# An encoder block on one core: Hyena products ahead of the conformer products, and five smaller changes of order

## The chip, the core and the metric

The kernel runs on one core of a Trainium2 chip. The metric is the device time of one execution in microseconds; before the change its median is 1410.63 us over three runs (1410.6 to 1410.8).

## The reference, cut to what matters

One layer on 256 tokens of width 2048, all in float32. `hy_*` and `cf_*` are the two branches, each of width 1024.

```python
h = rms_norm(x, mix_pre_g)
proj = h @ w_in                       # [hyena 3*1024 | cf_a | cf_b | gate_a | gate_b]
hy_in = depthwise_conv(hy_in, hy_conv_w, hy_conv_b)          # 3 taps
v, x1, x2 = split(hy_in)
kf = hyena_filters_freq(...)          # small MLP with sines, then a Fourier transform
z = x1 * fft_long_conv(v, kf[0]);  y_a = x2 * fft_long_conv(z, kf[1])
u = depthwise_conv(cf_a * sigmoid(cf_b), cf_dw_w, cf_dw_b)   # 31 taps
y_b = silu(layer_norm(u, cf_ln_g, cf_ln_b))
merged = sigmoid(gate_a) * (y_a @ hy_proj) + sigmoid(gate_b) * (y_b @ cf_proj)
x = x + rms_norm(merged @ w_out, mix_post_g)
h = rms_norm(x, ffn_pre_g)
x = x + rms_norm((silu(h @ w_gate) * (h @ w_up)) @ w_down, ffn_post_g)
```

## The kernel before, in words

**Products.** Every weight comes from memory once, in pieces of [128 x 2 x 512] (512 KB), by a load on SP's queue. `split_group` (line 281) lets ACT cast the piece to a rounded high part `hi` (line 299) and DVE subtract to get the low part `lo` (line 300). PE then does three products for each block of weights: activation high and low against `hi`, activation high against `lo`. There are four buffers for the raw piece and three each for `hi` and `lo`, so loads, splits and products of neighbouring groups overlap. All products go through the helper at line 87. `chunk_as` (line 355) makes a [256 x 512] result in two banks of PSUM, `main`: 8 groups of 12 products for a width of 2048, 4 groups for a width of 1024.

**Side work.** Everything else (filter, long convolutions, LayerNorm, evacuation of results) is written as generators. After each weight group the loop calls `pump(budget)` (line 108): it steps the generators in the queue until their stated costs use up the budget; `yield 1.2` states a cost, `yield None` ends the generator's turn until the next group. At most two of the generators in `side` are stepped in one turn. `drain` (line 134) steps given generators to their end at once. `before_chunk` and `after_chunk` keep at most one chunk's evacuation waiting. The program is then ordered by a scheduler (line 1246) that may move instructions where nothing pins them; `keep_in_program_order`, and `in_order` (line 197) for all calls on an engine, pin the instructions marked so among each other.

**Start.** Eight products of zeros run first (line 172) and one more in `first_chunk` (line 315), before the first weights. `x_norm` (line 459) loads x in four pieces, squares them on ACT (lines 272 and 469), forms rstd on DVE (`rsqrt`, line 223) and spreads it with a small product (line 450) to `rX`. `conv3` (line 724) needs `rX` to evacuate the first chunk (line 734). `filter_mlp` (line 496) waits six turns, loads five small arrays, and does two small products (lines 506 and 513), each followed by a sine (line 494).

**Middle.** After the six Hyena inputs and four conformer chunks come eight gate chunks (line 944), stored as sigmoids. Then, for each of four column chunks, the Hyena product (`hy_proj`), scaled by its gate (line 822), and the conformer product (`cf_proj`), merged with it (lines 928 and 929), transposed and split for the next product. The conformer branch ends at lines 863 and 867, and `layer_norm` (line 871) follows: statistics, rstd, normalization (line 881), and for each of four column pairs four transposes (line 892), sigmoid on ACT (line 899), an affine on DVE (line 900), a product (line 902), and the high and low part (lines 906 and 907) that `cf_proj` takes in. All that is left of `side` is drained behind the first Hyena product, in front of the first conformer product:

```python
    for n in range(4):
        before_chunk()
        after_chunk(scale_by(chunk_as(a["hy_proj"][n], yaT, 1.35), gates[n]))
        drain(side if n == 0 else [])
        before_chunk()
        mT.extend(slot([P, 2, 2, T], F32R) for _ in range(2))
        after_chunk(merge(chunk_as(a["cf_proj"][n], ybT, 1.35), gates[4 + n], gates[n], mT[-2:]))
```

**Products with a norm behind them.** `w_out` and `w_down` go through `product_as` (line 382): groups are one block of 128 rows and one half `hf` of the columns. The last eight groups (`late`) are split ahead into spare buffers, and their products are done token half by token half, piece by piece, so that each piece can be squared and scaled while the next is computed. After `w_out`, `turn` (line 1007) transposes the first token half, `turn_first` (line 1037) while the second half is still computed; `first_gate` (line 1064) starts the first FFN chunk with hand-placed products, and turns the second half in its loop, with `ahead` splitting weights ahead. `finish_block` (line 1136) writes the output in five pieces for each token half.

Of the kernel before, what the change touches and what calls it, by code (L numbers as in the profile page):

```python
# [15 lines left out]
ALU = mybir.AluOpType  # L16
AX = mybir.AxisListType

P = 128
# [34 lines left out]
def block_kernel(ctx: ExitStack, tc: tile.TileContext, a: dict, out: bass.AP):  # L54
# [248 lines left out]
    def first_chunk(act, budget, turn):  # L303


        ps = [psm.tile([P, 2, T], F32, tag="main", name=nm("main")) for _ in range(2)]
        kept = tc.keep_in_program_order
        groups = KT // 2
        ahead = deque()

        def split(g):
            ahead.append(split_group(a["w_in0"][g], on=(act_chain, dve_chain)))

        turn(0)
        keep_warm(1, zeros[:, 0:P], zeros)
        split(0)
        for g in range(groups):
            if g + 1 < groups:
                turn(g + 1)
                split(g + 1)  # L320
            hi, lo = ahead.popleft()
            for k in range(2):
                for c in range(4):
                    o = ps[c // 2][:, c % 2, :]
                    for s in range(2):
                        kept(mm(o, hi[:, k, c * P:(c + 1) * P], act[g][:, k, s, :],
                                g == 0 and k == 0 and s == 0 and c % 2 == 0, False))
            for k in range(2):
                for c in range(4):
                    kept(mm(ps[c // 2][:, c % 2, :], lo[:, k, c * P:(c + 1) * P],  # L330
                            act[g][:, k, 0, :], False, g == groups - 1 and k == 1))
            pump(budget)
        return ps
# [48 lines left out]
    def product_as(w, nkt, act, budget, late, done):  # L382

        ps = [[], []]
        first = 4
        groups = [(kt, hf) for hf in range(2) for kt in range(first)]
        groups += [(kt, hf) for kt in range(first, nkt) for hf in range(2)]

        def mms(kt, hf, t, hi, lo):
            av = act[kt // 2][:, kt % 2, :, t * P:(t + 1) * P]
            for j in range(2):
                o = ps[t][2 * hf + j]
                mm(o, av[:, 0, :], hi[:, j, :], kt == 0, False)
                mm(o, av[:, 1, :], hi[:, j, :], False, False)
            for j in range(2):
                mm(ps[t][2 * hf + j], av[:, 0, :], lo[:, j, :], False, kt == nkt - 1)

        held = []  # L400
        before_chunk()
        for i, (kt, hf) in enumerate(groups):
            if kt == 0:
                if hf:
                    drain(list(evac))
                    evac.clear()
                ps[0] += [aux() for _ in range(2)]
                ps[1] += [psm.tile([P, 512], F32, tag="main", name=nm("main")) for _ in range(2)]
            ahead = i >= len(groups) - late
            hi, lo = split_group(  # L410
                w[kt * P:(kt + 1) * P, hf * 1024:(hf + 1) * 1024].rearrange(
                    "p (j n) -> p j n", n=512), ahead)
            if ahead:
                held.append((kt, hf, hi, lo))
            else:
                for t in range(2):
                    mms(kt, hf, t, hi, lo)
                pump(budget)
        for t in range(2):
            for n in range(4):  # L420
                for kt, hf, hi, lo in held:
                    if hf == n // 2:
                        av = act[kt // 2][:, kt % 2, :, t * P:(t + 1) * P]
                        mm(ps[t][n], av[:, 0, :], hi[:, n % 2, :], False, False)
                        mm(ps[t][n], av[:, 1, :], hi[:, n % 2, :], False, False)
                        mm(ps[t][n], av[:, 0, :], lo[:, n % 2, :], False, kt == nkt - 1)
                done(t, n, ps[t][n])
# [29 lines left out]


    def x_norm():
        for _ in range(2):  # L460
            yield None
        for c in range(4):
            xs = slot([P, 2, 512])
            nc.sync.dma_start(
                xs, a["xm"][:, c * 512:(c + 1) * 512].rearrange("(t p) n -> p t n", p=P))
            for _ in range(2):
                yield None
            for t in range(2):
                tc.keep_in_program_order(half_mean_square(xs[:, t, :], ssx[:, t, c:c + 1]))
        yield 1.2  # L470
        for t in range(2):
            rms_rstd(rstd_x[:, t:t + 1], ssx[:, t, :], f"rx{t}")
        yield None
        per_token(rX, rstd_x, aux())
        done.add("x_norm")
# [18 lines left out]
        nc.scalar.activation(dst, u, AF.Sin)  # L494

    def filter_mlp():
        for _ in range(6):
            yield None
        nc.sync.dma_start(zT, a["zT"])
        nc.sync.dma_start(w1, a["w1"])  # L500
        nc.sync.dma_start(fp, a["fp"])
        for i in range(2):
            nc.sync.dma_start(w2d[:, i * FH:(i + 1) * FH], a["w2"])
        yield None
        ps = aux()
        tc.keep_in_program_order(nc.tensor.matmul(ps[:FH, :T], w1, zT, start=True, stop=True))
        h1 = scr[:FH, 2, :]
        sin_layer(h1, ps[:FH, :T], FH, 0)
        yield 1.9
        for _ in range(3):  # L510
            yield None
        ps = aux()
        tc.keep_in_program_order(nc.tensor.matmul(ps[:, :T], w2d, h1, start=True, stop=True))
        h2 = scr[:, 3, :]
        sin_layer(h2, ps[:, :T], P, 2)
        nc.scalar.copy(h2s, h2)
        nc.vector.tensor_tensor(out=h2s[FH:], in0=h2[FH:], in1=h2s[FH:], op=ALU.subtract)
        done.add("mlp")
        yield 2.2
# [351 lines left out]
    def layer_norm():  # L871
        while ("cf", 0) not in done or ("cf", 1) not in done:
            yield None
        for t in range(2):
            nc.vector.bn_aggr(out=mv[:, t, :], in_=stats[:, t])
        vv = sm([P, 2], "lnv", bufs=1)
        nc.vector.tensor_scalar(vv, mv[:, :, 1], EPS, 0.5, op0=ALU.add, op1=ALU.mult)
        rsqrt(rstd_c, vv, 2, "ln")
        yield 1.5
        for t in range(2):  # L880
            nc.vector.tensor_scalar(
                yt[t], yt[t], mv[:, t, 0:1], rstd_c[:, t:t + 1],
                op0=ALU.subtract, op1=ALU.mult)
            yield 0.6
        yield None
        yield from hold(3)
        for cp in range(4):
            ps = aux().rearrange("p (c t) -> p c t", t=T)
            for cc in range(2):
                c = 2 * cp + cc  # L890
                for t in range(2):
                    nc.tensor.transpose(
                        ps[:, cc, t * P:(t + 1) * P], yt[t][:, c * P:(c + 1) * P], ident)
            sg = t5([P, 2, T])
            lin = t5([P, 2, T])
            for cc in range(2):
                c = 2 * cp + cc
                g, b = pv[:, LN_G + c:LN_G + c + 1], pv[:, LN_B + c:LN_B + c + 1]
                nc.scalar.activation(sg[:, cc, :], ps[:, cc, :], AF.Sigmoid, bias=b, scale=g)
                nc.vector.tensor_scalar(lin[:, cc, :], ps[:, cc, :], g, b, op0=ALU.mult, op1=ALU.add)  # L900
            yb = t5([P, 2, T])
            nc.vector.tensor_tensor(out=yb, in0=lin, in1=sg, op=ALU.mult)
            yield 1.8
            d = slot([P, 2, 2, T], F32R)
            ybT.append(d)
            nc.scalar.copy(d[:, :, 0, :], yb)  # L906
            nc.vector.tensor_tensor(out=d[:, :, 1, :], in0=yb, in1=d[:, :, 0, :], op=ALU.subtract)
            yield 0.7
            yield None
        release(3)  # L910

    w_as = a["w_as"]
# [36 lines left out]
    for n in range(4):  # L949
        before_chunk()  # L950
        after_chunk(scale_by(chunk_as(a["hy_proj"][n], yaT, 1.35), gates[n]))
        drain(side if n == 0 else [])
        before_chunk()
        mT.extend(slot([P, 2, 2, T], F32R) for _ in range(2))
        after_chunk(merge(chunk_as(a["cf_proj"][n], ybT, 1.35), gates[4 + n], gates[n], mT[-2:]))
# [79 lines left out]
            second.append((og, rstd, last))  # L1035

    def turn_first(n):
        for i in {1: (0, 1), 2: (2, 3)}.get(n, ()):
            turn(0, (2 * i, 2 * i + 1))

    def turn_second(kp):
# [22 lines left out]
    def first_gate(w, budget):  # L1064
# [21 lines left out]
        mms(1, 0)  # L1086
        mms(2, 0, (0,))
        turn_second(0)
        ahead(3)
        mms(2, 0, (1,))  # L1090
        turn_second(1)
        ahead(4)
        mms(0, 1)
        for g in range(2, groups):
            turn_second(g)
            ahead(g + 3)
            mms(g - 1, 1)
            if g + 1 < groups:
                mms(g + 1, 0)
# [34 lines left out]
        after_chunk(glu(ps, sg, hid[-2:]))  # L1134

    def finish_block(t, og, rstd, last):
        for lo, hi in ((0, 256), (256, 512), (512, 1024), (1024, 1536), (1536, 2048)):
            c = slice(lo % 1024, lo % 1024 + hi - lo)
            xp = xr[t][lo // 1024][:, c]
            if lo == 1024:  # L1140
# [109 lines left out]
```

## Time and profile before

| | |
|---|---|
| median of three runs | 1410.63 us |
| the profiled execution | 1409.3 us |
| its span | 1407.4 us |
| mean granted clock of TensorE | 0.996 |
| busy: PE / DVE / ACT | 1387.4 / 868.0 / 669.3 us |
| moved from memory | 261.4 MB, 187 GB/s |
| share of PE in the chain that ended last | 94% |

A row of a timeline gives start, duration, engine, line, operation, output and inputs, how often, and in brackets how long the engine had stood idle and what it waited for. Records of consecutive products overlap, since their ends are modelled: the distance between starts is the time of one. [...] The span ends some microseconds after the last instruction of DVE, when the last store has landed.

### The profile page before, as it was taken

To read this page: it belongs to the slowest core of one execution; us is meant where nothing else is said; L and a number is where in the kernel's file an instruction comes from. 1 tells how busy PE (TensorE), PEld (TensorE's weight loads), DVE (VectorE), ACT (ScalarE), POOL (GpSimd) and SP (SyncE) were. 2 spreads that over 40 slices of the span, in tenths; PEclk is the share of its full clock that TensorE was granted. 3 is DMA by queue.
4 is the path that set the end of the run, shared out by engine and by line. 5 is a ranking of instruction groups with operands and counts; after the bars stand their busy time and mean duration, and the time that the engine had idled before them with its cause. 6 is when DMAs were issued, how large, how long until landed. Compare 5 with 4: busy or idle time off the path is not lost.

```text
span 1407.4 us, 16889 instructions
## 1 busy us (share of the span) xinstructions
PE 1387.4 (99%) x6435; PEld 1155.2 (82%) x6435; DVE 868.0 (62%) x1084; ACT 669.3 (48%) x844; POOL 11.2 (1%) x23
## 2 busy tenths in 40 slices
PE   9999999999999899999999999999999999999997
PEld 8788888888888778887788888888888888888886
DVE  6997977777777776547655445454455444444446
ACT  6665554444555444436644444444444444333343
POOL 0010000000000000000000000000000000000000
PEclk9999999999999999999999999999999999999999
DMA  9766555555554446765466666666666666556653
GB/s 347 217 200 179 177 180 166 169 158 152 169 169 153 162 137 191 265 199 195 133 211 188 189 193 191 184 192 186 194 189 191 186 221 193 193 189 194 195 188 134
DMA packets 76544, 264.58 MB, mean 188 GB/s; under 512 B 8689, under 2 KB 10002, under 8 KB 76464
## 3 DMA queue, kind: packets, MB, share of 16 engines
q1 hardware_dynamic: 75520, 261.74, 59.0%
q0 software_dynamic: 944, 1.77, 0.4%
q8 instruction: 50, 0.82, 0.2%
q14 instruction: 30, 0.25, 0.0%
HBM read 261.38 MB, written 2.10 MB: 187 GB/s over the span
## 4 chain that ended last, share of the span: by engine, by line
PE 94%; DVE 3%; DMA 2%; ACT 1%; issue 0%; DVEq 0%; SPq 0%; ACTq 0%
PE main L87 78%; PE aux L87 14%; DMA raw<-in_w_out_dram 1%; DVE big L201 1%; PE aux L1120 1%; DVE lo L300 0%; ACT hi L299 0%; DMA raw<-in_w_gu_dram 0%; DVE big L1004 0%; DVE big L300 0%; PE aux L704 0%; PE aux L620 0%; PE aux L937 0%; DMA big<-in_xT_dram 0%; ACT t L272 0%
## 5 line engine op out<-in xcount | busy, mean ns | idle before, releaser
L300 DVE TENSOR_TENSOR lo<-raw,hi 128x1024 fp32r<-128x1024 f32 x447 | 546.0, 1223 | 437.6 <-ACT hi L299 419.4
L299 ACT CAST hi<-raw 128x1024 fp32r<-128x1024 f32 x447 | 470.6, 1054 | 631.5 <-PE main L87 579.2
L87 PE MATMUL main<-hi,big 128*128 128x512 f32 x2824 | 716.8, 391 | 2.6 <-ACT big L906 2.1
L87 PEld LDWEIGHTS main<-hi,big 128*128 128x128 f32 x2824 | 528.7, 188 | 113.2 <-ACT big L906 2.4
L87 PE MATMUL main<-lo,big 128*128 128x512 f32 x1412 | 392.5, 390 | 0.0
L87 PEld LDWEIGHTS main<-lo,big 128*128 128x128 f32 x1412 | 265.1, 188 | 55.0
L87 PE MATMUL aux<-hi,big 128*128 128x512 f32 x416 | 111.9, 390 | 0.0
L87 PE MATMUL main<-big,hi 128*128 128x512 f32 (+1 forms) x448 | 99.3, 367 | 2.0 <-DVE t L734 1.2
L87 PEld LDWEIGHTS aux<-hi,big 128*128 128x128 f32 x416 | 77.9, 188 | 16.1
L87 PEld LDWEIGHTS main<-big,hi 128*128 128x128 f32 x448 | 75.0, 194 | 14.1 <-issue 2.0
L87 PE MATMUL aux<-big,big 128*128 128x512 f32 x288 | 77.0, 391 | 0.1
L87 PE MATMUL aux<-lo,big 128*128 128x512 f32 x208 | 64.3, 389 | 0.0
L87 PEld LDWEIGHTS aux<-big,big 128*128 128x128 f32 x288 | 53.6, 188 | 11.5 <-ACT big L299 0.5
L87 PEld LDWEIGHTS main<-big,lo 128*128 128x128 f32 x384 | 52.6, 192 | 3.4
L87 PE MATMUL main<-big,lo 128*128 128x256 f32 x384 | 54.3, 283 | 0.0
L87 PEld LDWEIGHTS aux<-lo,big 128*128 128x128 f32 x208 | 39.0, 188 | 8.1
L87 PE MATMUL main<-big,big 128*128 128x512 f32 x132 | 32.0, 393 | 0.0
L300 DVE TENSOR_TENSOR big<-raw,big 128x1024 fp32r<-128x1024 f32 x16 | 19.6, 1226 | 14.7 <-ACT big L299 14.7
L87 PEld LDWEIGHTS main<-big,big 128*128 128x128 f32 x132 | 24.5, 188 | 5.0
L299 ACT CAST big<-raw 128x1024 fp32r<-128x1024 f32 x16 | 16.8, 1052 | 18.3 <-DMA raw<-in_w_out_dram 9.4
L816 DVE SCALAR_TENSOR_TENSOR big<-main,rstd,big 128x512 f32<-128x512 f32 x22 | 15.5, 747 | 11.9 <-PE main L87 11.9
L662 ACT CAST big<-t 128x512 fp32r<-128x512 f32 x24 | 14.6, 618 | 5.3 <-DVE t L661 5.3
(212 smaller groups left out, 627.9 us busy)
## 6 DMA issues: line engine op xcount, KB each, us to landing
raw<-in_w_gu_dram SPq DMA_DIRECT2D x176, 512.0 KB
raw<-in_w_as_dram SPq DMA_DIRECT2D x96, 512.0 KB
raw<-in_w_down_dram SPq DMA_DIRECT2D x88, 512.0 KB
raw<-in_w_in_dram SPq DMA_DIRECT2D x44, 512.0 KB
raw<-in_w_out_dram SPq DMA_DIRECT2D x32, 512.0 KB
raw<-in_hy_proj_dram SPq DMA_DIRECT2D x16, 512.0 KB
raw<-in_cf_proj_dram SPq DMA_DIRECT2D x16, 512.0 KB
raw<-in_w_in_dram SPq DMA_DIRECT2D x8, 256.0 KB
```

The costliest lines, as they stand in the source:

```text
L87: return nc.tensor.matmul(o, lhsT, rhs, start=start, stop=stop, skip_group_check=True)
L201: return lambda *p, **k: tc.keep_in_program_order(getattr(eng, name)(*p, **k))
L299: S.copy(hi[:, k], raw[:, k])
L300: V.tensor_tensor(out=lo[:, k], in0=raw[:, k], in1=hi[:, k], op=ALU.subtract)
L662: nc.scalar.copy(rs[j][ft][:, 0], v)
L816: nc.vector.scalar_tensor_tensor(out=d[:, t], in0=ps[t], scalar=scale[t], in1=d[:, t], op0=ALU.mult, op1=ALU.mult)
L1120: nc.tensor.transpose(tr[:, c, t * P:(t + 1) * P], sg[:, t, f:f + P], ident)
```

## The change

1. In the mixer all four Hyena products (`hy_proj`) now come first, then the rest of the side work is drained, then all four conformer products with their merges.
2. The LayerNorm's transposes and its ACT and DVE instructions are pinned to source order; it has one more turn of waiting behind rstd and one in each column pair between transposes and sigmoid (there in place of the one at the pair's end), and other stated costs.
3. The norm of x starts one turn sooner; the filter's MLP starts three turns later and waits one turn more between its layers.
4. Four warm-up products in place of one in front of the first chunk.
5. The last eight groups of `w_out` and `w_down` are ordered column half by column half, not row block by row block.
6. In `w_out` the last pair of transposed blocks of the first token half (6 and 7) moves from the end of the product into the loop of `first_gate` (at g = 3), where weights are split two groups ahead and not three.
7. The output of a token half is written in pieces of 512, 512, 512, 256 and 256 columns and not of 256, 256, 512, 512 and 512.

```diff
@@ -312,7 +312,7 @@
             ahead.append(split_group(a["w_in0"][g], on=(act_chain, dve_chain)))
 
         turn(0)
-        keep_warm(1, zeros[:, 0:P], zeros)
+        keep_warm(4, zeros[:, 0:P], zeros)
         split(0)
         for g in range(groups):
             if g + 1 < groups:
@@ -386,7 +386,9 @@
         ps = [[], []]
         first = 4
         groups = [(kt, hf) for hf in range(2) for kt in range(first)]
-        groups += [(kt, hf) for kt in range(first, nkt) for hf in range(2)]
+        last = nkt - late // 2
+        groups += [(kt, hf) for kt in range(first, last) for hf in range(2)]
+        groups += [(kt, hf) for hf in range(2) for kt in range(last, nkt)]
 
         def mms(kt, hf, t, hi, lo):
             av = act[kt // 2][:, kt % 2, :, t * P:(t + 1) * P]
@@ -457,8 +459,7 @@
 
 
     def x_norm():
-        for _ in range(2):
-            yield None
+        yield None
         for c in range(4):
             xs = slot([P, 2, 512])
             nc.sync.dma_start(
@@ -494,7 +495,7 @@
         nc.scalar.activation(dst, u, AF.Sin)
 
     def filter_mlp():
-        for _ in range(6):
+        for _ in range(9):
             yield None
         nc.sync.dma_start(zT, a["zT"])
         nc.sync.dma_start(w1, a["w1"])
@@ -507,7 +508,7 @@
         h1 = scr[:FH, 2, :]
         sin_layer(h1, ps[:FH, :T], FH, 0)
         yield 1.9
-        for _ in range(3):
+        for _ in range(4):
             yield None
         ps = aux()
         tc.keep_in_program_order(nc.tensor.matmul(ps[:, :T], w2d, h1, start=True, stop=True))
@@ -871,17 +872,20 @@
     def layer_norm():
         while ("cf", 0) not in done or ("cf", 1) not in done:
             yield None
+        kept = tc.keep_in_program_order
+        S, V = in_order(nc.scalar), in_order(nc.vector)
         for t in range(2):
             nc.vector.bn_aggr(out=mv[:, t, :], in_=stats[:, t])
         vv = sm([P, 2], "lnv", bufs=1)
         nc.vector.tensor_scalar(vv, mv[:, :, 1], EPS, 0.5, op0=ALU.add, op1=ALU.mult)
         rsqrt(rstd_c, vv, 2, "ln")
-        yield 1.5
+        yield 2.5
+        yield None
         for t in range(2):
-            nc.vector.tensor_scalar(
+            V.tensor_scalar(
                 yt[t], yt[t], mv[:, t, 0:1], rstd_c[:, t:t + 1],
                 op0=ALU.subtract, op1=ALU.mult)
-            yield 0.6
+            yield 0.8
         yield None
         yield from hold(3)
         for cp in range(4):
@@ -889,24 +893,24 @@
             for cc in range(2):
                 c = 2 * cp + cc
                 for t in range(2):
-                    nc.tensor.transpose(
-                        ps[:, cc, t * P:(t + 1) * P], yt[t][:, c * P:(c + 1) * P], ident)
+                    kept(nc.tensor.transpose(
+                        ps[:, cc, t * P:(t + 1) * P], yt[t][:, c * P:(c + 1) * P], ident))
             sg = t5([P, 2, T])
             lin = t5([P, 2, T])
+            yield None
             for cc in range(2):
                 c = 2 * cp + cc
                 g, b = pv[:, LN_G + c:LN_G + c + 1], pv[:, LN_B + c:LN_B + c + 1]
-                nc.scalar.activation(sg[:, cc, :], ps[:, cc, :], AF.Sigmoid, bias=b, scale=g)
-                nc.vector.tensor_scalar(lin[:, cc, :], ps[:, cc, :], g, b, op0=ALU.mult, op1=ALU.add)
+                S.activation(sg[:, cc, :], ps[:, cc, :], AF.Sigmoid, bias=b, scale=g)
+                V.tensor_scalar(lin[:, cc, :], ps[:, cc, :], g, b, op0=ALU.mult, op1=ALU.add)
+            yield 1.1
             yb = t5([P, 2, T])
-            nc.vector.tensor_tensor(out=yb, in0=lin, in1=sg, op=ALU.mult)
-            yield 1.8
+            V.tensor_tensor(out=yb, in0=lin, in1=sg, op=ALU.mult)
             d = slot([P, 2, 2, T], F32R)
             ybT.append(d)
-            nc.scalar.copy(d[:, :, 0, :], yb)
-            nc.vector.tensor_tensor(out=d[:, :, 1, :], in0=yb, in1=d[:, :, 0, :], op=ALU.subtract)
-            yield 0.7
-            yield None
+            S.copy(d[:, :, 0, :], yb)
+            V.tensor_tensor(out=d[:, :, 1, :], in0=yb, in1=d[:, :, 0, :], op=ALU.subtract)
+            yield 1.4
         release(3)
 
     w_as = a["w_as"]
@@ -949,7 +953,8 @@
     for n in range(4):
         before_chunk()
         after_chunk(scale_by(chunk_as(a["hy_proj"][n], yaT, 1.35), gates[n]))
-        drain(side if n == 0 else [])
+    drain(side)
+    for n in range(4):
         before_chunk()
         mT.extend(slot([P, 2, 2, T], F32R) for _ in range(2))
         after_chunk(merge(chunk_as(a["cf_proj"][n], ybT, 1.35), gates[4 + n], gates[n], mT[-2:]))
@@ -1035,7 +1040,7 @@
             second.append((og, rstd, last))
 
     def turn_first(n):
-        for i in {1: (0, 1), 2: (2, 3)}.get(n, ()):
+        for i in {1: (0, 1), 2: (2,)}.get(n, ()):
             turn(0, (2 * i, 2 * i + 1))
 
     def turn_second(kp):
@@ -1086,14 +1091,15 @@
         mms(1, 0)
         mms(2, 0, (0,))
         turn_second(0)
-        ahead(3)
         mms(2, 0, (1,))
         turn_second(1)
-        ahead(4)
+        ahead(3)
         mms(0, 1)
         for g in range(2, groups):
             turn_second(g)
-            ahead(g + 3)
+            ahead(g + 2)
+            if g == 3:
+                turn(0, (6, 7))
             mms(g - 1, 1)
             if g + 1 < groups:
                 mms(g + 1, 0)
@@ -1134,7 +1140,7 @@
         after_chunk(glu(ps, sg, hid[-2:]))
 
     def finish_block(t, og, rstd, last):
-        for lo, hi in ((0, 256), (256, 512), (512, 1024), (1024, 1536), (1536, 2048)):
+        for lo, hi in ((0, 512), (512, 1024), (1024, 1536), (1536, 1792), (1792, 2048)):
             c = slice(lo % 1024, lo % 1024 + hi - lo)
             xp = xr[t][lo // 1024][:, c]
             if lo == 1024:
```

## Rows read from the trace of the kernel before

**Rows 1.** the page, busy time by engine over the span (us, share, instructions)
```profile
PE 1387.4 (99%) x6435; PEld 1155.2 (82%) x6435; DVE 868.0 (62%) x1084; ACT 669.3 (48%) x844; POOL 11.2 (1%) x23
```

**Rows 2.** waits of PE (us in total, times, longest us)
```profile
PE aux L892 <- DVE big L881: 3.5, 1, 3.5
PE main L87 <- ACT big L906: 2.1, 1, 2.1
...
PE main L87 <- DVE t L734: 1.2, 1, 1.2
```

**Rows 3.** timeline of PE at the LayerNorm (start us, us, what, xcount, idle before it)
```profile
470.77 1.98 PE L87 MATMUL main<-hi,big 128*128 128x512 f32 x8
...
484.15 1.07 PE L87 MATMUL main<-lo,big 128*128 128x512 f32 x4
488.69 3.40 PE L892 MATMUL aux<-ident,big 128*128 128x128 f32 x16 [3.47 <-DVE big L881]
494.23 3.56 PE L87 MATMUL main<-hi,big 128*128 128x512 f32 x8 [2.14 <-ACT big L906]
...
498.94 2.01 PE L87 MATMUL main<-hi,big 128*128 128x512 f32 x8
...
501.69 1.98 PE L87 MATMUL main<-hi,big 128*128 128x512 f32 x8
```

**Rows 4.** stretches of 1 us at the LayerNorm (length, busy by engine, PEclk, DMA)
```profile
490.00:491.00 1.00, 1.00 (x7) 1.00 (x6) 0.00 (x0) 0.52 (x1) 0.00 (x0) 0.50 0.46 172
...
496.00:497.00 1.00, 1.00 (x4) 0.81 (x3) 0.78 (x3) 0.88 (x2) 0.00 (x0) 0.50 0.00 0
```

**Rows 5.** timeline of DVE: end of the Hyena branch, end of the conformer branch
```profile
402.18 0.69 DVE L783 TENSOR_TENSOR big<-t,big 128x512 fp32r<-128x512 f32 x1
...
477.57 0.69 DVE L863 TENSOR_TENSOR big<-t,aux 128x512 f32<-128x512 f32 x1 [2.38 <-PE aux L87]
```

**Rows 6.** timeline of ACT at the LayerNorm
```profile
490.48 0.56 ACT L899 ACTIVATE t<-aux,pv 128x256 f32<-128x256 f32 x1 [5.08 <-PE aux L892]
```

**Rows 7.** groups of instructions, 440 to 640 us (busy us, mean ns, idle before)
```profile
L300 DVE TENSOR_TENSOR lo<-raw,hi 128x1024 fp32r<-128x1024 f32 x64 | 77.9, 1221 | 50.5 <-ACT hi L299 46.3 <-PE main L87 4.2
...
L928 DVE TENSOR_TENSOR big<-main,big 128x512 f32<-128x512 f32 x8 | 5.1, 685 | 2.9 <-PE main L87 2.9
```

**Rows 8.** timeline of ACT at the norm of x
```profile
37.81 1.28 ACT L494 ACT_TABLE_LOAD   x1
39.11 0.42 ACT L494 ACTIVATE big<-big 64x256 f32<-64x256 f32 x1
39.43 0.61 ACT L272 ACTIVATE t<-big 128x512 f32<-128x512 f32 x1
```

**Rows 9.** timeline of PE at the norm of x
```profile
44.01 0.79 PE L450 MATMUL aux<-diag,ones 128*128 128x128 f32 x4 [0.77 <-DVE rstdx L239]
...
46.65 1.17 PE L87 MATMUL main<-big,hi 128*128 128x512 f32 x4 [1.23 <-DVE t L734]
```

**Rows 10.** timeline of PE at the start
```profile
1.33 4.21 PE L87 MATMUL aux<-big 128*128 128x512 f32 x9 [1.33 <-POOL big L163]
6.14 3.79 PE L87 MATMUL main<-big,hi 128*128 128x256 f32 x16 [0.60 <-ACT hi L217]
...
10.99 1.24 PE L87 MATMUL main<-big,hi 128*128 128x256 f32 x9
```

**Rows 11.** timeline of ACT at the start
```profile
9.23 1.05 ACT L217 CAST hi<-raw 128x1024 fp32r<-128x1024 f32 x1 [1.13 <-DMA raw<-in_w_in_dram]
```

**Rows 12.** timeline of DVE where `w_out` hands over to the FFN
```profile
667.08 2.15 DVE L201 SCALAR_TENSOR_TENSOR big<-aux,pv,big 128x128 fp32r<-128x128 f32 x8
```

**Rows 13.** timeline of PE where `w_out` hands over to the FFN
```profile
660.33 1.62 PE L1015 MATMUL aux<-ident,big 128*128 128x128 f32 x8 [0.34 <-DVE big L1004]
...
670.45 0.44 PE L1015 MATMUL aux<-ident,big 128*128 128x128 f32 x2 [0.56 <-DVE big L1004]
```

**Rows 14.** timeline of DVE at the end
```profile
1402.33 1.41 DVE L1142 SCALAR_TENSOR_TENSOR big<-big,pdr,big 128x512 f32<-128x512 f32 x2
```

## The prediction

> **What bounds the kernel now.** I read the page's busy times first: PE is busy for 1387.4 us of a span of 1407.4 [rows 1], so all the change can win lies in 20 us of PE idle time, and in stretches where PE is busy but slow. Next the waits of PE: the largest are at the LayerNorm, 3.5 us and 2.1 us, then 1.2 us at the short convolution [rows 2]. Then the timeline at each of these places, and the granted clock in stretches of 1 us. With the waits of [rows 3, 9, 10, 13] taken off (10.4 us), some 9.6 us of the idle time are left; they lie almost all behind the last product, where nothing can fill them.
>
> At the LayerNorm the reader is to see a hole: after the four products at 484.15 the next ones start at 494.23, and between them stand only 16 transposes [rows 3]. [...]
>
> The profiled execution took 1409.3 us, 1.3 less than the median of the runs, 1410.63. I make the sum as a difference and take it off the median. A difference over 0.2% (2.8 us) is about what a measurement of this kernel can tell from no change.
>
> **The change part by part.**
>
> **Hyena products first.** Every product stays, 16 weight groups of each branch on SP's queue, only their order changes. Removed is the hole: four products from 484.15 end at 484.15 + 4 x 0.229 = 485.07; to 494.23 that is 9.16 us. The 16 transposes remain; they took 3.40 us at half the level, so 1.7 us. Idle 7.5 us, plus 4.71 - 2.75 = 1.96 us of slow products: 9.4 us. What hides the LayerNorm now is three chunks of Hyena products, 3 x 48 x 0.229 = 33 us, which end at about 485 + 33 = 518. Today the first column pair is ready at 494.23, 24 us sooner. Four added turns of waiting in the filter may shift the side work by 4 x 2.75 = 11 us; that leaves 13 us. In the code's own costs the new LayerNorm asks 2.5 + 2 x 0.8 + 4 x 2.5 = 14.1, and 12 groups at 1.35 give 16.2, less 4 x 1.4 for scaling: some 10.6 net of evacuation, so the last pair or two are drained in front of the first conformer product. That product's first group needs only the first pair, each later group (12 x 0.229 = 2.75 us) one pair more, so this is covered. The Hyena inputs are ready at 402.87 [rows 5], the first Hyena product stands at 470.77 [rows 3]: 68 us of cover against 11. I take -9.4; if the cover is gone the hole comes back whole, 0.
>
> **LayerNorm in source order.** The same instructions, but ACT and DVE may no longer pull its pieces past each other. Behind a sigmoid that waits for transposes stand ACT's casts, and behind these PE. Today ACT waited 5.08 us at the first sigmoid [rows 6]. The turn added between transposes and sigmoid gives PE a whole group, 2.75 us, to get there. I take 0; the other end is a rival.
>
> **Merges close together.** Four merges follow each other without a Hyena chunk between. Per chunk DVE needs 4 splits x 1.22 and six operations of 0.69 [rows 7], 4.9 + 4.1 = 9.0 us, against 11.0 us of products: covered, 0.
>
> **Norm of x ahead of the filter.** One turn less ahead of the four loads of x on SP; the filter's five small loads, its two products and its sine follow later. Today the last square of x starts at 39.43, behind the sine's table load at 37.81 and the sine at 39.11 [rows 8], and PE then stands 0.77 and 1.23 us [rows 9]. Without load and sine the squares start 39.43 - 37.81 = 1.6 us sooner, with the earlier load at most a group (2.75 us) sooner, which covers both waits: -2.0 at best. The filter's DVE work moves into the next products; nothing in the trace prices that there, so I bound it by the waits that it could renew, 0 to 2.0. I take 0.3, since it is the same work under the same products: -1.7 net, ends 0 and -2.0. The load-to-sine distance here is 39.11 - 37.81 = 1.30 us. [...]
>
> **Four warm-up products in place of one.** [...] Ends +0.3 and -0.7.
>
> **Handover of w_out to the FFN.** The last eight groups come half by half, so the first two pieces of the first token half finish before the last weights are in, and their squares with them. Eight transposes become four there, and DVE loses half of the 2.15 us that stand ahead of the second half's rstd [rows 12]. PE waits 0.34 and 0.56 us there [rows 13]. Against it, weights are split one group less ahead, and the moved pair adds work in the fourth turn. Ends -0.9 and +1.0 (one more wait of that size); I take -0.6, nearest to the waits that lose their cause.
>
> **Last stores.** The same elements in the same five operations. Two 512-column operations take 1.41 us [rows 14]; the half of the last one leaves 0.35 us sooner, and the last store carries 128 KB in place of 256 KB. No row prices that store. Ends 0 and -0.7 (the operation itself); I take -0.3.
>
> Sum: -9.4 - 1.7 - 0.7 - 0.6 - 0.3 = -12.7, so 1410.6 - 12.7 = 1397.9 us. The best ends give -13.7, 1396.9; all small terms at their worse ends (0, +0.3, +1.0, 0) give -8.1, 1402.5.
>
> **The rivals.**
>
> **The small orders have no effect.** The program's scheduler may place the sine, the loads and the splits where it did before; then only the order of the products counts, and the last stores: -9.4 - 0.3, 1400.9 us. For it speaks that the whole program goes through a scheduler that orders what the source doesn't pin (line 1246). Against it: the squares, the filter's products and the LayerNorm's pieces are pinned.
>
> **The hole moves along.** If the second conformer half comes so late that it is drained with the whole LayerNorm after the fourth Hyena chunk, PE stands there as now: -12.7 + 9.4 = -3.3, 1407.3 us. It decides when the side work slips by over 24 us; counted are 11.
>
> **A waiting sigmoid blocks the casts (slower).** Each of four column pairs puts a sigmoid at the head of ACT. If PE reaches the transposes only after the group whose cast stands behind that sigmoid, every pair stops PE as the first does now: 494.23 - 490.48 = 3.75 us [rows 3, 6], plus 1.96 us at the low level. Four times 5.7 is 22.8: -12.7 + 22.8 = +10.1, 1420.7 us. It decides from the point where two sigmoids (1.0), the copy (0.6) and a cast (1.05) no longer fit in the 2.75 us of a group; that is 2.65, so it is near if all of a pair fall into one group, but a pair spreads over two turns. [...]
>
> **How the numbers follow.** The forecast has 0.72, the small orders without effect 0.14, the moved hole 0.07, the blocked casts 0.04, and 0.03 are for a result near no change from causes that I don't see. Range 1395.5 to 1405: the best end less the 1.3 us by which executions differ, up past the worse ends and the first rival; the hole that moves lies outside. Faster by over 0.2% means under 1407.8: 0.72 + 0.14 + 0.04 (half of the moved hole) = 0.90; within 0.2%: 0.06; slower: 0.04.
>
> **What would show it.** Right: no wait of PE at the LayerNorm's transposes, a granted clock of 1.00 from the start of the products to the last one, the squares of x ahead of the sine on ACT, the second weight group on PE before 10.6 us, and about 12 to 13 us less span with the same matmul count. Wrong: a hole ahead of the first conformer product, several waits of PE for casts among the Hyena products, or a new wait among the four merges.

## The result, and the profile after

The changed kernel takes 1398.97 us (median of four runs, 1398.54 to 1399.35) against 1410.62 us before (four runs, 1409.11 to 1410.8): a ratio of 0.992, 95% interval 0.9903 to 0.9937. It is 11.65 us faster; forecast were 12.7. The profiled executions took 1399.35 and 1409.3 us, so the two traces differ by 9.95 us, and the steps below are measured against that.

The busy times of the page after, to be read beside [rows 1]:

```profile
PE 1384.8 (99%) x6438; PEld 1153.3 (83%) x6438; DVE 867.2 (62%) x1084; ACT 669.2 (48%) x844; POOL 11.9 (1%) x23
```

PE has the three more warm-up products and is still 2.6 us less busy; its mean granted clock is 0.997 against 0.996. The waits of PE after (us in total, times, longest), beside [rows 2]:

```profile
PE main L87 <- ACT big L201: 1.2, 1, 1.2
...
PE main L87 <- DVE big L201: 0.4, 1, 0.4
```

The waits of 3.5 us at the LayerNorm's transposes and of 1.2 us at the short convolution are gone. (Instructions pinned with `in_order` now stand under its line, 201.) Two new ones are there, 1.2 us for ACT and 0.4 us for DVE. The timeline of PE shows where, behind the last Hyena group, beside [rows 3]:

```profile
468.64 1.98 PE L87 MATMUL main<-hi,big 128*128 128x512 f32 x8
...
510.13 0.60 PE L896 MATMUL aux<-ident,big 128*128 128x128 f32 x4
...
516.06 1.47 PE L896 MATMUL aux<-ident,big 128*128 128x128 f32 x12
517.29 2.08 PE L87 MATMUL main<-hi,big 128*128 128x512 f32 x8
519.21 1.07 PE L87 MATMUL main<-lo,big 128*128 128x512 f32 x4
521.52 0.73 PE L87 MATMUL main<-hi,big 128*128 128x512 f32 x2 [1.24 <-ACT big L201]
522.61 2.85 PE L87 MATMUL main<-hi,big 128*128 128x512 f32 x6 [0.35 <-DVE big L201]
...
526.64 2.57 PE L87 MATMUL main<-hi,big 128*128 128x512 f32 x10
```

Only one column pair is transposed among the Hyena products (510.13). The other three are transposed together at 516.06, just in front of the first conformer group at 517.29, so its second group needs a pair whose LayerNorm has only begun. That group takes 526.64 - 521.52 = 5.12 us, not the 12 x 0.229 = 2.75 us of a group at full level (granted clock 1.00, 498.94 to 501.69 in [rows 3]). The stretch of 1 us behind the wait (columns as in [rows 4]) shows that the granted clock fell as well:

```profile
523.00:524.00 1.00, 1.00 (x4) 0.71 (x4) 0.37 (x2) 0.56 (x1) 0.00 (x0) 0.50 0.56 176
```

Why the second pair is late is seen on DVE, here from the second pair's first affine to its low part, with the scaling and the splits that stand between:

```profile
516.03 1.29 DVE L823 TENSOR_TENSOR big<-main,big 128x512 f32<-128x512 f32 x2 [0.21 <-PE main L87]
517.24 1.22 DVE L300 TENSOR_TENSOR lo<-raw,hi 128x1024 fp32r<-128x1024 f32 x1
518.37 0.54 DVE L201 TENSOR_SCALAR t<-aux,pv 128x256 f32<-128x256 f32 x1
...
520.73 1.22 DVE L300 TENSOR_TENSOR lo<-raw,hi 128x1024 fp32r<-128x1024 f32 x1
521.87 0.68 DVE L201 TENSOR_TENSOR big<-t,big 128x512 fp32r<-128x512 f32 x1
```

ACT and DVE take turns over one pair, and each turn of DVE queues behind a split or the gate's scaling. On ACT:

```profile
516.70 0.57 ACT L201 ACTIVATE t<-aux,pv 128x256 f32<-128x256 f32 x1 [0.25 <-PE aux L896]
518.94 0.56 ACT L201 ACTIVATE t<-aux,pv 128x256 f32<-128x256 f32 x1 [1.68 <-DVE t L201]
519.46 1.05 ACT L299 CAST hi<-raw 128x1024 fp32r<-128x1024 f32 x1
```

From the first sigmoid at 516.70 to the end of the low part at 521.87 + 0.68 a pair takes 5.85 us, where a group lasts 2.75. The Hyena chunks' budget of 1.35 left three pairs to this place.

To account for the rest I compare starts on PE. Before, the rows that [rows 3, 9, 10] don't hold:

```profile
28.26 2.08 PE L87 MATMUL main<-big,hi 128*128 128x256 f32 x16
...
641.77 10.97 PE L87 MATMUL aux<-big,big 128*128 128x512 f32 x46
652.57 7.42 PE L87 MATMUL main<-big,big 128*128 128x512 f32 x32
...
697.47 2.11 PE L87 MATMUL main<-hi,big 128*128 128x512 f32 x8 [0.22 <-ACT hi L299]
```

And after:

```profile
10.75 2.18 PE L87 MATMUL main<-big,hi 128*128 128x256 f32 x16 [0.45 <-ACT hi L217]
...
28.42 3.79 PE L87 MATMUL main<-big,hi 128*128 128x256 f32 x23
...
43.79 2.00 PE L87 MATMUL main<-big,hi 128*128 128x512 f32 x8
...
644.73 7.42 PE L87 MATMUL main<-big,big 128*128 128x512 f32 x32
...
660.38 0.38 PE L1020 MATMUL aux<-ident,big 128*128 128x128 f32 x2
...
687.23 2.11 PE L87 MATMUL main<-hi,big 128*128 128x512 f32 x8 [0.19 <-ACT hi L299]
```

| start of | before | after | difference |
|---|---|---|---|
| second weight group | 10.99 | 10.75 | -0.24 |
| last group of the first chunk | 28.26 | 28.42 | +0.16 |
| half chunk behind the norm of x | 46.65 | 43.79 | -2.86 |
| first Hyena product | 470.77 | 468.64 | -2.13 |
| held products of `w_out`'s second half | 652.57 | 644.73 | -7.84 |
| first regular FFN group | 697.47 | 687.23 | -10.24 |
| the whole span | 1407.4 | 1397.5 | -9.9 |

So the LayerNorm's stretch gave -5.7, the handover -2.4, the norm of x -3.0 with 0.7 given back behind it, and the start nothing.

### The profile page after: what moved, and what is told of

The parts are those of the page before. It is cut to its first block, busy times and chain, and to the rows that moved or that the text cites. A ratio compares the mean times of both kernels' runs of the same rounds, so it can differ in the third digit from the quotient of the medians.

```text
span 1397.5 us, 16896 instructions
## 1 busy us (share of the span) xinstructions
PE 1384.8 (99%) x6438; PEld 1153.3 (83%) x6438; DVE 867.2 (62%) x1084; ACT 669.2 (48%) x844; POOL 11.9 (1%) x23
## 4 chain that ended last, share of the span: by engine, by line
PE 98%; DVE 1%; DMA 0%; ACT 0%; SPq 0%; issue 0%; DVEq 0%; ACTq 0%
PE main L87 80%; PE aux L87 16%; PE aux L1126 1%; DMA raw<-in_w_in_dram 0%; PE aux L705 0%; PE aux L941 0%; PE aux L621 0%; PE aux L1020 0%; PE aux L578 0%; DVE big L1148 0%; DVE lo L300 0%; ACT t L272 0%; ACT hi L299 0%; SPq L156 0%; DVE t L201 0%
```

## The experiments

The theory on trial: the order of the products carries the gain, and what is left of the hole comes from side work that is late and drained in one piece. The rivals (pinning, blocked casts, the other five edits) stand in each expectation. All diffs are against the changed kernel, but for the order alone, which is against the kernel before. Ratios are to the median of the kernel before on the same chip: 1409.4 us for the order put back, the LayerNorm as it was, the larger budget and the early filter; 1410.35 for the handover, the last groups, the one warm-up product and the larger budget with the old last groups; 1409.71 for the other four. Times of runs from different groups are best compared by these ratios.

**The order put back.**

```diff
-    drain(side)
-    for n in range(4):
+        drain(side if n == 0 else [])
```

> The changed kernel (1398.97 us) with only the order of the two branches' products put back: Hyena and conformer chunks alternate and the side work is drained behind the first Hyena chunk. Theory A (the three Hyena chunks in between hide the LayerNorm): the hole comes back, and is at least as large as the 9.4 us of before, since the filter now starts later; less the 3.8 us that the changed kernel still loses there, that is 5 to 10 us more, 1404 to 1409. Rival B (the pinned LayerNorm made the gain): under 1401.

Measured: 1408.58 us, ratio 0.9994 (0.9984 to 1.0004). The hole is back whole and larger, now 6.1 us of it one wait at the transposes (timeline of PE):

```profile
488.40 0.48 PE L896 MATMUL aux<-ident,big 128*128 128x128 f32 x1 [6.11 <-DVE big L201]
...
493.81 3.78 PE L87 MATMUL main<-hi,big 128*128 128x512 f32 x8 [1.23 <-ACT big L201]
```

From the first Hyena product (467.87) to the held products of `w_out` (654.29) it takes 186.4 us, before 652.57 - 470.77 = 181.8. Without item 1 the other six items together gain nothing that can be measured: what the norm of x and the handover win, the later LayerNorm takes.

**The order alone**, put into the kernel before.

```diff
-        drain(side if n == 0 else [])
+    drain(side)
+    for n in range(4):
```

> The kernel before with only the Hyena products put ahead of the conformer products; LayerNorm unpinned, filter early, all else as before. Theory A (the three Hyena chunks hide the LayerNorm, and what the changed kernel still lost there comes from the later filter): no wait of PE at the LayerNorm's transposes or behind them, all of 9 to 10 us gained, 1400.5 to 1401.5 against 1410.5. Rival B (pins are needed): a wait of 1 us or more left, 1403 or more.

Measured: 1401.81 us, ratio 0.9943 (0.9929 to 0.9956). Timeline of PE: half chunk, first Hyena product, first transposes, the products of `w_out`:

```profile
46.77 2.04 PE L87 MATMUL main<-big,hi 128*128 128x512 f32 x4 [1.23 <-DVE t L734]
...
472.25 1.98 PE L87 MATMUL main<-hi,big 128*128 128x512 f32 x8
...
494.70 0.27 PE L892 MATMUL aux<-ident,big 128*128 128x128 f32 x1
...
633.98 10.62 PE L87 MATMUL aux<-big,big 128*128 128x512 f32 x46
644.44 7.42 PE L87 MATMUL main<-big,big 128*128 128x512 f32 x32
```

No wait stands at the transposes. The held products come 8.13 us sooner than before, though the first Hyena product came 1.48 us later: -9.6 across the LayerNorm. Of this 0.34 lies in the 46 products ahead of them (644.44 - 633.98 = 10.46 against 652.57 - 641.77 = 10.80); the rest, -9.3, is the term that was forecast as -9.4. Most of the 1.48 us were lost where [rows 9] have the wait of 1.23: here the first four products behind it took 48.61 - 46.77 = 1.84 us, against 1.01 before. The granted clock was 0.50 (stretch of this trace, columns as in [rows 4]), where the kernel before has 1.00:

```profile
47.00:48.00 1.00, 1.00 (x3) 0.81 (x4) 1.00 (x5) 1.00 (x4) 0.00 (x0) 0.50 0.76 238
```

In time the order alone gives 7.9 us; the changed kernel on the same chip, at 1398.31, gives 11.4. So the other items are worth some 3.5 us once the order is there.

**The LayerNorm as it was** (unpinned, with its old costs and turns; the order stays).

```diff
-        yield 2.5
-        yield None
+        yield 1.5
...
-                    kept(nc.tensor.transpose(
+                    nc.tensor.transpose(
...
-            yield None
...
-                S.activation(sg[:, cc, :], ps[:, cc, :], AF.Sigmoid, bias=b, scale=g)
+                nc.scalar.activation(sg[:, cc, :], ps[:, cc, :], AF.Sigmoid, bias=b, scale=g)
```

> The changed kernel with the LayerNorm as it was before (no pins, old stated costs and turns), all else kept. Theory A (the order of the products carries the gain, the pins little): within 1 us of 1399. Rival B (the pins make the remaining wait of 1.24 us and the low level behind it): both vanish, about 1395.5. Rival C (the unpinned pieces gather in front of the conformer products as before): a larger hole, 1402 to 1405.

Measured: 1396.11 us, ratio 0.9905 (0.9889 to 0.9922). One wait of 0.28 us is left in this place (timeline of PE):

```profile
503.29 0.27 PE L893 MATMUL aux<-ident,big 128*128 128x128 f32 x1
...
522.86 2.60 PE L87 MATMUL main<-hi,big 128*128 128x512 f32 x10 [0.28 <-ACT hi L299]
```

The first transposes come at 503.29, not 510.13. I had expected a time within 1 us of 1399. So the new LayerNorm is no cover here but a cost of 2 to 3 us; the run doesn't tell its pins from its added turns and costs, which were undone together.

**A larger budget under the Hyena products**, 2.2 for 1.35.

```diff
-        after_chunk(scale_by(chunk_as(a["hy_proj"][n], yaT, 1.35), gates[n]))
+        after_chunk(scale_by(chunk_as(a["hy_proj"][n], yaT, 2.2), gates[n]))
```

> The changed kernel with a budget of 2.2 and not 1.35 per weight group in the four Hyena chunks, so that the LayerNorm is stepped faster there. Theory A (the last three pairs stand directly in front of the first conformer product because the side work ran out of turns): they come out among the Hyena products, the wait of 1.24 us and the low level behind it vanish, 1395 to 1396. Rival B (pinned pieces block the casts of the Hyena products): new waits of PE for casts, 1399 or more.

Measured: 1395.54 us, ratio 0.9902 (0.9888 to 0.9917). The transposes spread over the Hyena products, from 495.17 to 508.73 (timeline of PE), and no wait of PE is left at the LayerNorm:

```profile
495.17 0.27 PE L896 MATMUL aux<-ident,big 128*128 128x128 f32 x1
...
502.22 0.60 PE L896 MATMUL aux<-ident,big 128*128 128x128 f32 x4
...
508.13 0.60 PE L896 MATMUL aux<-ident,big 128*128 128x128 f32 x4
```

Same pins, same operations, only drawn sooner: the rest of the hole was lateness. Behind the first chunk PE's waits for `hi` come to 0.4 us in all, so the casts weren't blocked.

**The filter as early as before.**

```diff
-        for _ in range(9):
+        for _ in range(6):
...
-            for _ in range(4):
+            for _ in range(3):
```

> The changed kernel with the filter's waiting turns as before (six and three), the norm of x still one turn sooner. Theory A (the remaining hole comes from the later filter; the norm of x gains by not standing behind the sine): the hole at the LayerNorm goes (-3.8), the first wait at the short convolution comes back (+2 to +3): 1397 to 1399, with the squares behind the sine again. Rival B (the sooner load alone made the gain at the norm of x): no wait there, 1395 to 1396.

Measured: 1398.1 us, ratio 0.992 (0.9905 to 0.9935), no different from the changed kernel. The LayerNorm comes sooner and no wait is left there, but the old wait at the short convolution is back, longer (PE: `45.16`, 2.03 us for L735). My reason for the norm of x, that the squares stood behind the sine, isn't enough: here the squares are done by 33.0 and the sine's table load starts only at 40.04, and PE waits all the same. What is late is DVE's queue. From its timeline, the first and last step of rstd and what stands between:

```profile
32.41 0.21 DVE L248 TENSOR_SCALAR rx0h<-rx0h,ssx 128x1 f32<-128x1 f32 x1 [0.84 <-ACT t L272]
...
34.45 1.21 DVE L300 TENSOR_TENSOR lo<-raw,hi 128x1024 fp32r<-128x1024 f32 x1
...
36.19 0.41 DVE L492 SCALAR_TENSOR_TENSOR big<-big 64x256 f32<-64x256 f32 x1
...
37.33 1.21 DVE L300 TENSOR_TENSOR lo<-raw,hi 128x1024 fp32r<-128x1024 f32 x1
...
38.80 0.14 DVE L239 SCALAR_TENSOR_TENSOR rstdx<-rx1t,rx1y 128x1 f32<-128x1 f32 x1
```

The chain takes 38.94 - 32.41 = 6.5 us, with the sine's range reduction and two splits drawn into it. Behind it stand more splits: to the first operation of L735 at 44.27 it takes another 5.3 us, in the changed kernel 38.04 - 34.74 = 3.3. There the chain of rstd runs unbroken (timeline of DVE):

```profile
32.67 0.21 DVE L248 TENSOR_SCALAR rx0h<-rx0h,ssx 128x1 f32<-128x1 f32 x1
...
34.58 0.16 DVE L239 SCALAR_TENSOR_TENSOR rstdx<-rx1t,rx1y 128x1 f32<-128x1 f32 x1
```

That is 2.1 us; in the kernel before, with one split between, it was 3.8 (40.17 to 43.93). So the later filter does two opposite things: it clears DVE for the norm, and it makes the LayerNorm late.

**The handover as before** (item 6 undone).

```diff
-        for i in {1: (0, 1), 2: (2,)}.get(n, ()):
+        for i in {1: (0, 1), 2: (2, 3)}.get(n, ()):
...
-            ahead(g + 2)
-            if g == 3:
-                turn(0, (6, 7))
+            ahead(g + 3)
```

> The changed kernel with the handover of w_out to the FFN as before (four pairs turned by the end of w_out, weights split three groups ahead), the last groups still column half by column half. Theory A (the moved pair and the shorter lead free DVE in front of the second half's rstd): the 2.7 us won between 600 and 720 us are lost again for the most part, +1.5 to +2.7 against the changed kernel. Rival B (the earlier first pieces of w_out carry it): within 0.6 us of the changed kernel.

Measured: 1400.64 us, ratio 0.9931 (0.9913 to 0.9949). DVE has its eight operations in a row again, and PE waits for what stands behind them (timelines of DVE and of PE):

```profile
657.47 2.15 DVE L201 SCALAR_TENSOR_TENSOR big<-aux,pv,big 128x128 fp32r<-128x128 f32 x8
```

```profile
660.84 0.44 PE L1020 MATMUL aux<-ident,big 128*128 128x128 f32 x2 [0.54 <-DVE big L1009]
```

From the held products to the first regular FFN group it takes 687.87 - 644.04 = 43.83 us; the changed kernel takes 687.23 - 644.73 = 42.50, the kernel before 44.90. Item 6 carries 1.3 of the 2.4 us.

**The last groups in the order of before** (item 5 undone).

```diff
-        last = nkt - late // 2
-        groups += [(kt, hf) for kt in range(first, last) for hf in range(2)]
-        groups += [(kt, hf) for hf in range(2) for kt in range(last, nkt)]
+        groups += [(kt, hf) for kt in range(first, nkt) for hf in range(2)]
```

> The changed kernel with the last eight groups of w_out and w_down in the order of before (row block by row block). Theory A (the new order lets the first pieces finish sooner): +0.5 to +1.5 at the handover, and the 0.3 us wait in the last products of w_down goes. Rival B (the new order only makes PE wait for the late halves): no loss at the handover, -0.3 to -1 in all.

Measured: 1398.75 us, ratio 0.9917 (0.99 to 0.9933), the time of the changed kernel. The same stretch takes 685.69 - 642.82 = 42.87 us, so item 5 carries some 0.4 of the handover's gain, and the time shows no gain. One place where it may lose as much are the 46 held products of `w_down`: 1377.55 - 1366.83 = 10.72 us in the changed kernel's trace, 10.42 here. But over all traces they take 10.46 to 11.54 us with the new order and 10.42 to 10.86 with the old one, so a cost of the order there isn't shown.

**One warm-up product again.**

```diff
-        keep_warm(4, zeros[:, 0:P], zeros)
+        keep_warm(1, zeros[:, 0:P], zeros)
```

> The changed kernel with one warm-up product in place of four. Theory A (the sooner full level is spent waiting for the second group's weights and activations): first products at the low level until 10 us, but the half chunk behind the first chunk starts within 0.3 us of where it does now; total within 0.5 us. Rival B (my forecast's term): +0.7 and more.

Measured: 1399.31 us, ratio 0.9921 (0.9905 to 0.9936). Timeline of PE at the start, beside [rows 10]:

```profile
1.33 3.73 PE L87 MATMUL aux<-big 128*128 128x512 f32 x9 [1.33 <-POOL big L163]
6.32 2.40 PE L87 MATMUL main<-big,hi 128*128 128x256 f32 x16 [1.27 <-ACT hi L217]
```

With nine products and a longer pause than in [rows 10] the first real products ran near full level (2.40 us for 16, not 3.79; the second group's 16 take 2.17). The second group starts at 10.20, against 10.75 and 11.27 in two executions of the changed kernel and 10.99 before: the three added products decide nothing here.

**The larger budget with the last groups as before** (both diffs above).

> The kernel with budget 2.2 in the Hyena chunks (1395.54 us) and the last eight groups in the order of before. Theory A (the column-half order makes PE wait 0.9 us in the last products of w_down where loads come late, and gains less at the handover): 1394.5 to 1395.3. Rival B (the order is worth more at the handover than it costs at the end): 1396 or more.

Measured: 1396.57 us, ratio 0.99 (0.9884 to 0.9917). PE waits 1.00 us at the first transposes of the handover (648.41, for DVE L1007), a wait that the larger budget with the new order has in neither of its two traces. In the next run, which has the new order there too, it is 0.54 (647.98). So item 5 may pay 0.5 to 1 us there; the times don't show it, since the runs overlap (1395.01 to 1397.57 here, 1395.27 to 1395.69 for the larger budget alone, on another chip).

**The larger budget, new order of the last groups for `w_out` alone** (the budget's diff above, and this).

```diff
-        last = nkt - late // 2
+        last = nkt - late // 2 if nkt == KT else nkt
```

> Budget 2.2 in the Hyena chunks, the new order of the last eight groups for w_out alone, the old one for w_down. Theory A (the column-half order pays at w_out, where a long chain of norm and transposes hangs on the first pieces, and costs at w_down, where PE waits for the late halves): 0.4 to 0.9 us under the same kernel with both in the new order, some 1395. Rival B (the waits at w_down depend on how the loads fall, not on the order): the same within 0.3.

Measured: 1394.99 us, ratio 0.9894 (0.9881 to 0.9908). It is 0.4 us under the larger budget alone (next), inside the spread of the runs (1394.24 to 1395.66 and 1394.41 to 1395.91), and the 46 held products of `w_down`, 10.42 us here, take 10.46 and 11.33 in the two traces of that one: undecided.

**The changed kernel and the larger budget once more**, side by side on one chip.

> The changed kernel itself once more, beside the others on one chip: 1398.5 to 1399.5.

> Budget 2.2 in the Hyena chunks once more, beside the changed kernel on one chip. Theory A: 3 to 4 us under the changed kernel. Rival B (the 1395.5 of the first time was the chip): within 1 us of it.

Measured: 1398.31 us, ratio 0.9918 (0.9905 to 0.9932), and 1395.39 us, ratio 0.9896 (0.9883 to 0.991). All runs of the one lie between 1397.72 and 1399.18, of the other between 1394.41 and 1395.91: the larger budget beats both kernels, by 2.9 and by 14.3 us.

The second trace of the changed kernel tells what the clock costs at the second conformer group. The waits are the same, but the granted clock stays at 1.00, and the group takes 525.55 - 521.62 = 3.93 us, not 5.12 (timeline of PE, and a stretch with columns as in [rows 4]):

```profile
521.62 0.73 PE L87 MATMUL main<-hi,big 128*128 128x512 f32 x2 [1.24 <-ACT big L201]
...
525.55 2.57 PE L87 MATMUL main<-hi,big 128*128 128x512 f32 x10 [0.25 <-ACT hi L299]
```

```profile
523.00:524.00 1.00, 1.00 (x6) 0.78 (x6) 0.37 (x2) 0.56 (x1) 0.00 (x0) 1.00 0.52 160
```

## Why the prediction was right, and where its steps were not

The time lay 1.1 us above the forecast, inside the range, and the mechanism is the one that was put first: the order of the products, worth 7.9 of 11.4 us when it stands alone, and without which the rest gains nothing. But that the sum came so close is in part luck: its terms have errors of both signs, and by the two traces the steps add up to -9.9, 2.8 short of the forecast. (The execution profiled before was 1.3 us under its median, the one after 0.4 over.)

Of the signs that the prediction named, three came: no wait at the LayerNorm's transposes, the squares of x ahead of the sine (the last at 32.02, the table load at 55.66), and a count that differs only by the three warm-up products. Three did not: the granted clock fell to 0.50 at 523, the second weight group started at 10.75 and not before 10.6, and the span is 9.9 us shorter, not 12 to 13.

- **Hyena products first, -9.4.** The price of the hole was right: the order alone gives -9.3. (Its 4.71 us for twelve slow products lie between the starts 494.23 and 498.94 of [rows 3]. For the transposes 1.7 us were reckoned; in this change four and twelve of them take 510.49 - 510.13 and 517.29 - 516.06, 1.6 us together.) What failed in this change is the step "the last pair or two are drained in front of the first conformer product [...] so this is covered". Three pairs were drained there, and a pair takes 5.85 us, not a group's 2.75, since DVE's splits and scalings stand in its chain. Left of the hole are 521.52 - (519.21 + 4 x 0.229) = 1.4 us ahead of the second group and 5.12 - 2.75 = 2.4 us in it: 3.8, so -5.6; the starts give -5.7, of which 0.37 lie, as with the order alone, in the 46 products ahead of `w_out`'s second half (644.73 - 634.30 = 10.43 us). Of the 3.8 some 1.2 us are the clock's luck (3.93 us for the same group in the second trace). The shift of the side work was sized rightly: forecast 11, and the conformer branch ends on DVE at 488.61 instead of the 477.57 of [rows 5]. It was the 10.6 net of evacuation, stated costs taken for time, that hid the lateness.
- **LayerNorm in source order, 0.** It costs 2 to 3 us in this surrounding. ACT does stand idle at a pinned sigmoid (1.68 us ahead of 518.94), but that held back no cast: a cast starts some 0.2 us behind a group's products with `hi` (509.42 behind 509.22), and those ahead of the next cast, which starts at 519.46, were done at 519.21. PE waits for the pair.
- **Merges, 0.** Right: PE has no wait there.
- **Norm of x, -1.7.** Measured -3.0 up to the half chunk: the two waits of [rows 9] are gone (2.0), and a small filter product (0.70 us in the kernel before, at 44.73) now runs later, at 66.23, which accounts for most of the 0.7 given back by the first Hyena product. Net -2.3. The reason was not enough: with the squares ahead of table load and sine the wait is still there when rstd's steps on DVE are drawn apart. The sizes were off as well: the square at 39.43 was the last but one (another starts at 40.04), and the squares end 8 us sooner, at 32.64 and not at 40.66, where 1.6 for the sine and at most 2.75 for the load were counted. The table load again took 1.28 us with the sine right behind (55.66, 56.96).
- **Warm-up, -0.7.** Nothing, and no run shows the term or its other end, +0.3. The first real products started at 6.74 and not at 6.14, and 16 of them took 2.60 us and not 3.79; the second group came 0.24 us sooner and the last group of the first chunk 0.16 later. With one product it was no worse.
- **Handover, -0.6.** Measured -2.4: item 6 carries 1.3 and item 5 0.4; 0.7 are not assigned. PE lost both waits of [rows 13] (660.38 stands without one), and DVE's row of eight became four:

```profile
657.91 1.12 DVE L201 SCALAR_TENSOR_TENSOR big<-aux,pv,big 128x128 fp32r<-128x128 f32 x4
```

- **Last stores, -0.3.** Nothing: from the last square on ACT to the end of the span it takes 1397.5 - 1388.63 = 8.87 us, before 1407.4 - 1398.58 = 8.82.

The rivals: the small orders had their effect, the hole moved along by two fifths (3.8 of 9.4), and no cast was blocked: PE's waits for `hi` behind the first chunk are 0.4 us in all. Whether a waiting sigmoid holds back a cast that stands behind it is not shown: no cast was ready in the idle 1.68 us, nor in the 5.08 us of [rows 6], where the products ahead of the next cast, at 497.88, started only at 494.23.

## What to carry to other kernels

When work is moved to hide a stall, count when the hidden work will really be finished: the length of its chain through the queues of all engines that it shares, not the sum of its stated costs. A change that delays the same side work elsewhere (here the filter, which clears DVE for the norm) spends the cover that another part of the change has just bought, and the budget by which side work is drawn has to be set anew for the new order: one number, 1.35 to 2.2, was worth 2.9 us here. Short dependent steps on a shared engine should not be queued among long ones; the same rstd took 2.1 us alone and 6.5 us among a sine's pieces and splits.

## What the hardware showed that I had not expected

The granted clock doesn't follow from the waits alone. In the changed kernel it fell to 0.50 behind waits of 1.24 and 0.35 us, and with the handover as before, behind 1.24 and 0.36 us, the group took 525.81 - 520.87 = 4.94 us, nearly as long; in the second trace of the very same kernel, and with the last groups as before, the same two waits left the clock at 1.00 (stretch of the latter trace, columns as in [rows 4]):

```profile
523.00:524.00 1.00, 1.00 (x6) 0.84 (x5) 0.97 (x2) 0.37 (x1) 0.00 (x0) 1.00 0.80 311
```

Likewise the wait of 1.23 us at the norm of x was followed by 1.00 in the kernel before and by 0.50 with the order alone. At the start, too, the level differs: 16 real products behind nine warm-up products took 3.79 us in the kernel before and 2.40 us with one warm-up product again. (This is read from the products' times; in the kernel before the profile's granted clock reads 1.00 there all the same.) I didn't find what decides. A single profile thus carries a luck of 1.2 to 1.4 us at each such place: 5.12 against 3.93 us at the second conformer group, 3.79 against 2.40 us at the start.
